# Three shared accumulator banks, a later closing and a third raw buffer in the forgetting stage of a hybrid decoder layer

## The chip, the cores and the metric

The kernel runs on one core of a Trainium2 chip. A core has TensorE (PE in the profile; matmuls, with the loads of their weights on a line of their own, PEld), VectorE (DVE), ScalarE (ACT), GpSimd (POOL) and SyncE (SP), which here only issues DMA transfers. Each engine runs its instructions in the order in which they stand; engines wait for each other by semaphores. Matmuls write to PSUM, which the kernel uses as eight banks of 128 x 512 fp32 numbers; everything else lies in SBUF (on the chip) or in DRAM. The metric is the device time of one execution in microseconds (us), the median of three runs.

## The reference

One decoder layer on a sequence of 1024 tokens with a model width of 1024:

```python
# in outline
h = rmsnorm(x, g)                                  # x (1, 1024, 1024)
q, k, v, ig, fg, fq, fk, fv, ff = split(h @ w_in)   # mLSTM: 4 heads of 128; forgetting attention: 8 heads of 64
a = mlstm_chunkwise(q, k, v, ig, log_sigmoid(fg))   # chunks of 64; q, k behind a causal convolution, a gated and normed
b = forgetting_attention(fq, fk, fv, log_sigmoid(ff))
x = x + concat(a, b) @ w_out
x = x + cross_attention(rmsnorm(x), rmsnorm(mem), w_q, w_kv, w_o)    # 256 memory tokens, 4 heads of 256
x = x + squared_relu_mlp(rmsnorm(x))
return rmsnorm(x, g_final)

def forgetting_attention(q, k, v, lf):              # per block of 128 queries
    s = q @ k.T * 64 ** -0.5
    s = s + (cumsum(lf)[query] - cumsum(lf)[key])   # decay
    s = where(query >= key, s, -inf)
    return softmax(s) @ v
```

All of it is in fp32. The kernel gets that precision by splitting a number into a high part, rounded to the matmul's format, and a low part, the rest; a product is three matmuls (lo x hi, hi x lo, hi x hi).

## The kernel before

The layer runs in stages: the input projections, the mLSTM, the forgetting attention, the output projection with its residual, the cross attention, the MLP, the final norm. The change is in the forgetting stage, which lasts from about 395 to 605 us of the span.

**Work of the stage.** Eight heads, each in two halves of 512 queries. Of a half there are four blocks of 128 queries (class `Tile`), each with its scores against all earlier keys, in parts of at most 512 keys. Per part:

- `score`: two matmuls (L734, L735) of stacked high and low parts into one of three banks `sc`.
- `top`: VectorE's negated row maximum (L741, or L744 with the causal mask).
- `exp`: ScalarE's exponential (L756) with the row's sum as a by-product; where there are two parts a tiny second one (L758).
- `scale`: VectorE makes the reciprocal of the sum (L763, L764), GpSimd multiplies the probabilities by it (L767).

For the output there are 96 value steps (class `Values`), one for each half of a head and each block `j` of 128 keys:

- `turn`: TensorE transposes the probabilities into a bank `tp` (L782).
- `cut`: split of the transposed probabilities into high (ScalarE, L134) and low (VectorE, L135).
- `add`: two matmuls (L801) that add this key block's part of the output to the half's sum. Values are loaded from DRAM (`fvd`, L849).
- `fx_close` when the half is done: the sum's bank holds the output's two parts in its upper and lower 64 partitions; ScalarE copies the upper one to SBUF (L810, `r_c<-ov`) and VectorE adds the lower one to it (L811, `r_f<-ov,r_c`).
- `fx_store` when both heads of a pair are done: the split of the result, and two stores to `mix` (L823, L824).

**Slots.** A function `slot` makes one round of all this: one turn, the adds of the value step two rounds back (`LAG`), the tops of the part that was scored in the round before, the cut, then closings, the exponentials of the parts topped in the round before, the scales, the loads, a score, and then side products. `in_order` fixes that order on every engine, SyncE's issues included: inside the stage nothing overtakes anything on its engine. The score of a slot takes the bank of `sc` whose exponentials stand in the slot before, so TensorE cannot run more than a slot ahead of ScalarE. The value steps follow the scores 13 slots behind (`LEAD_`). Slots are counted here from the first with a value step, which begins with its turn on TensorE.

**Side products.** The rest of a slot's TensorE time goes to matmuls that later stages need, pieced in by a rate (`RATE` 4.6 a slot): keys and values of the cross attention (`key_unit`, `value_unit`) and then the output projection (`out_unit`, 16 units of 128 output columns by 512 tokens, which read the stored `mix` back in pieces, `mix_step`, L934). When a unit is done its `sink` empties its bank a slot later: L885 (keys), L137 and L138 (values), L956 (output projection). Its weights come in raw, by `raw_load` (L975, `wr<-w_out_a`, 320 KB each for the output projection), two buffers `wr` taking turns, and are split in two halves by `cut_half` (L988 ScalarE; L989 the low part, GpSimd for the first half, VectorE for the second). A new raw is asked for in the slot after its buffer was cut.

**Banks.** Three `sc`, two `tp`, one `mm`, one `m2` (in the trace `m`) and one `ov`. In the stage every half's sum is in `ov`, while side products alternate between `mm` and `m2`. In the slot after a closing has been started, no adds are made (`closing`), and the slot after that makes up for them with four; so the next half's sum does not ask for `ov` while the closing reads it.

## Time and profile before

The median of three runs is 1521.66 us (1521.24 to 1523.61).

| | |
|---|---|
| profiled execution, its own time | 1523.35 us |
| its span on the core | 1521.6 us |
| granted TensorE clock | 0.998 |
| TensorE busy, whole span | 1502.7 us |
| VectorE, ScalarE, GpSimd busy | 1100.3, 727.7, 510.1 us |
| forgetting stage, 395 to 605 us: TensorE busy | 204.82 of 210.00 us |
| there VectorE, ScalarE, GpSimd busy | 161.39, 148.75, 94.91 us |

How to read the rows that follow: a row of the timeline has the start, the length, the engine, the line, the operation, what it writes and from what (by the program's names), shapes, and in brackets the idle time of the engine ahead of it and what ended that. Matmuls overlap: the next starts before the former has ended, so a row's length is more than its share of time. A row of a group has the count, then total busy time and mean length in ns, then the idle time ahead of all of its instructions.

### The profile page before, as it was taken

The numbers are of one execution on the slowest core, as the hardware profiler recorded it, in microseconds if no ns is written. First come the engines' busy times: TensorE is split into PE (matmuls) and PEld (weight loads), VectorE is DVE, ScalarE is ACT, GpSimd is POOL, SyncE is SP. The second block draws the span as 40 slices with busy tenths as digits, with TensorE's granted clock in tenths as the row PEclk, the third lists the DMA queues.
The fourth block names the chain that finished last, engine by engine and source line by source line (L and its number), as shares of the span: only waits on it lengthen the run. The fifth ranks groups of instructions, "written<-read, shape, count | busy, mean of one in ns | idle before, by whom it ended". The sixth has DMA issues, their size and how long they took to land.

```text
span 1521.6 us, 21977 instructions
## 1 busy us (share of the span) xinstructions
PE 1502.7 (99%) x7694; PEld 1261.5 (83%) x7694; DVE 1100.3 (72%) x1743; ACT 727.7 (48%) x1360; POOL 510.1 (34%) x543
## 2 busy tenths in 40 slices
PE   9999999999999999999999999999999999999997
PEld 9988888889999788888888877778787888888887
DVE  7766676765787786944457989898887667787665
ACT  7324343334687665644443456666664621122124
POOL 1003030413364442511110034544555265663322
PEclk9999999999999999999999999999999999999999
DMA  6322223435888886843344437776678777776623
GB/s 239 109 77 87 98 100 114 135 126 157 246 244 267 260 264 230 300 131 124 119 147 157 153 134 277 247 256 242 222 252 286 291 277 276 276 270 248 239 94 111
DMA packets 122538, 299.86 MB, mean 197 GB/s; under 512 B 13614, under 2 KB 28264, under 8 KB 115516
## 3 DMA queue, kind: packets, MB, share of 16 engines
q1 hardware_dynamic: 122428, 298.46, 57.4%
q8 instruction: 60, 0.98, 0.3%
q14 instruction: 50, 0.41, 0.1%
HBM read 199.60 MB, written 98.81 MB: 196 GB/s over the span
## 4 chain that ended last, share of the span: by engine, by line
PE 93%; DVE 3%; ACT 2%; DMA 1%; issue 1%; SPq 0%; DVEq 0%; POOLq 0%; POOL 0%; ACTq 0%
PE tp L186 8%; PE tp L187 8%; PE tp L188 8%; PE m L186 6%; PE sc L186 6%; PE m L187 6%; PE m L188 6%; PE sc L187 6%; PE sc L188 6%; PE mm L186 6%; PE mm L187 6%; PE mm L188 6%; PE ov L186 2%; PE ov L187 2%; PE ov L188 2%; PE ov L801 2%
## 5 line engine op out<-in xcount | busy, mean ns | idle before, releaser
L186 PE MATMUL tp<-act,wl 128*128 128x512 f32 (+1 forms) x440 | 172.9, 393 | 1.2 <-ACT row L1396 0.7
L187 PE MATMUL tp<-act,wh 128*128 128x512 f32 (+1 forms) x440 | 172.1, 391 | 0.0
L188 PE MATMUL tp<-act,wh 128*128 128x512 f32 (+1 forms) x440 | 171.7, 391 | 0.0
L135 DVE TENSOR_TENSOR wl<-wr,wh 128x1024 fp32r<-128x1024 f32 (+2 forms) x95 | 124.5, 1311 | 22.0 <-ACT wh L134 21.4
L134 ACT ACTIVATE wh<-wr 128x1024 fp32r<-128x1024 f32 (+2 forms) x95 | 95.6, 1007 | 75.9 <-PE tp L188 34.7
L186 PE MATMUL mm<-act,wl 128*128 128x512 f32 (+1 forms) x332 | 127.5, 384 | 0.0
L188 PE MATMUL mm<-act,wh 128*128 128x512 f32 (+1 forms) x332 | 127.3, 383 | 0.0
L187 PE MATMUL mm<-act,wh 128*128 128x512 f32 (+1 forms) x332 | 127.2, 383 | 0.0
L186 PE MATMUL m<-act,wl 128*128 128x512 f32 (+1 forms) x308 | 117.7, 382 | 0.5 <-DVE wl L135 0.5
L188 PE MATMUL m<-act,wh 128*128 128x512 f32 (+1 forms) x308 | 117.7, 382 | 0.0
L187 PE MATMUL m<-act,wh 128*128 128x512 f32 (+1 forms) x308 | 117.5, 381 | 0.0
L186 PEld LDWEIGHTS tp<-act,wl 128*128 128x128 f32 x440 | 82.6, 188 | 20.6 <-ACT row L1396 1.2
L188 PEld LDWEIGHTS tp<-act,wh 128*128 128x128 f32 x440 | 82.6, 188 | 18.9
L187 PEld LDWEIGHTS tp<-act,wh 128*128 128x128 f32 x440 | 82.7, 188 | 18.5
L186 PE MATMUL sc<-act,wl 128*128 128x512 f32 (+1 forms) x248 | 97.0, 391 | 1.0 <-DVE wl L135 1.0
L188 PE MATMUL sc<-act,wh 128*128 128x512 f32 (+1 forms) x248 | 96.7, 390 | 0.0
L187 PE MATMUL sc<-act,wh 128*128 128x512 f32 (+1 forms) x248 | 96.6, 390 | 0.0
L1467 POOL TENSOR_TENSOR z<-wr 128x256 f32<-128x256 f32 x56 | 51.7, 944 | 130.6 <-DMA wr<-w_ff2q 116.8
L134 ACT ACTIVATE wh<-z 128x1024 fp32r<-128x1024 f32 (+1 forms) x54 | 55.5, 1028 | 80.8 <-POOL z L1467 58.4
L135 DVE TENSOR_TENSOR wl<-z,wh 128x1024 fp32r<-128x1024 f32 (+1 forms) x54 | 74.3, 1376 | 7.8 <-ACT wh L134 7.6
L134 ACT ACTIVATE w<-wr 128x768 fp32r<-128x768 f32 (+2 forms) x31 | 25.5, 823 | 106.2 <-PE tp L186 33.7
L188 PEld LDWEIGHTS mm<-act,wh 128*128 128x128 f32 x332 | 62.3, 188 | 12.7
(726 smaller groups left out, 4288.4 us busy)
## 6 DMA issues: line engine op xcount, KB each, us to landing
act<-right SPq DMA_DIRECT2D x49, 1024.0 KB
right<-w SPq DMA_DIRECT2D x56, 256.0 KB
wr<-w_ff2q SPq DMA_DIRECT2D x28, 512.0 KB
right<-r_d SPq DMA_DIRECT2D x49, 256.0 KB
right<-r_e SPq DMA_DIRECT2D x49, 256.0 KB
act<-fqk SPq DMA_DIRECT2D x48, 256.0 KB
wr<-w_in SPq DMA_DIRECT2D x20, 512.0 KB
wr<-w_ff SPq DMA_DIRECT2D x20, 512.0 KB
```

What stands on the lines that cost most here:

```text
L134: s.activation(hi, src, AF.Copy)
L135: return v.tensor_tensor(out=lo, in0=src, in1=hi.bitcast(F32), op=ALU.subtract)
L186: nc.tensor.matmul(ps, w[1], x[0], start=first, stop=False, skip_group_check=more)
L187: nc.tensor.matmul(ps, w[0], x[1], start=False, stop=False, skip_group_check=more)
L188: nc.tensor.matmul(ps, w[0], x[0], start=False, stop=last, skip_group_check=more)
L801: nc.tensor.matmul(self.ov[:, c0:], self.fv[:, self.j], t[:, c0:], start=self.j == 0 and t is self.p[1], stop=self.last and t is self.p[0])
L1467: g.tensor_tensor(out=o, in0=x, in1=y, op=op)
```

## The change

Three things are changed, all in the forgetting stage.

1. **Banks.** A list `spares` holds `mm`, `m2` and `ov`. The first add of a half and the start of a side product take the bank at its head (`bank_of`); it is put back at its end (`bank_back`) when the closing's addition or the sink has been issued. Adds are no longer left out after a closing: two are made in each slot.
2. **Closing.** ScalarE's copy comes after the exponentials of its slot; VectorE's addition comes in the next slot, after the tops and ahead of the cut. The bank goes back then, and a pair's split and stores come a slot later too.
3. **Raws.** Of the 16 raws of the output projection, numbers 1, 4, 7, 10 and 13 go to a free part of the buffer `row` instead of `wr`. The load of number 0 also issues that of number 1, so that three are under way.

```diff
+    spares, sums = ["mm", "m2", "ov"], {}
+    def bank_of(use):
+        tag = spares.pop(0)
+        sums[use] = ps_tile(tag), tag
+        return sums[use][0]
+    def bank_back(use):
+        spares.append(sums.pop(use)[1])
...
         def add(self):
             c0 = min(self.d0 * P, 256)
+            if self.j == 0:
+                bank_of((self.hd, self.hf))
+            ov = sums[self.hd, self.hf][0]
...
-    def fx_close(hd, hf, ov):
+    def fx_close(hd, hf):
+        ov = sums[hd, hf][0]
...
         s.activation(t[0:FXD], ov[FXD:], AF.Copy)
-        v.tensor_tensor(out=om[hf][rng], in0=ov[0:FXD], in1=t[0:FXD], op=ALU.add)
+        def finish():
+            v.tensor_tensor(out=om[hf][rng], in0=ov[0:FXD], in1=t[0:FXD], op=ALU.add)
+            bank_back((hd, hf))
+            if hd % 2:
+                stores.append((hd, hf, True))
+        return finish
...
-            ps = mm()
+            ps = bank_of("unit")
...
             v.tensor_tensor(out=t[:, 1], in0=ps[:, :NM], in1=row_m, op=ALU.mult)
+            bank_back("unit")
...
-            raw = sb("wr", [P, 1024], 2)[:, : src.shape[-1]]
+            c, m = src.shape[-1], n - len(sources) + 2 * KT
+            raw = row[:, NM : NM + c] if m > 0 and m % 3 == 1 else sb("wr", [P, 1024], 2)[:, :c]
             last_raw[:] = [load(raw, src)]
             raws_.append(raw)
             ages.append(now[1])
+            if m == 0:
+                raw_load()
...
-            closing = bool(ended)
-            ended.clear()
...
-            while adds and not closing and len(adds) >= (LAG if x else 1):
+            while adds and len(adds) >= (LAG if x else 1):
...
             for t, e in tops:
                 t.top(e)
+            while closed:
+                closed.pop(0)()
             if x:
                 x.cut()
                 adds.append(x)
-            for hd, hf, ov in ended:
-                fx_close(hd, hf, ov)
-                if hd % 2:
-                    stores.append((hd, hf, True))
             exps = topped[:]
             topped[:] = tops
             for t, e in exps:
                 t.exp(e)
+            while ended:
+                closed.append(fx_close(*ended.pop(0)))
```

Lines move with it: the turn is L792 after, the add L814, the closing's copy L824, its addition L827, the reads of mix L956, the sinks L905 (keys) and L978 (output projection), the raw's load L999, the first line of a cut half L1014. What each slot holds of side products is the same in both programs.

TensorE in the slot after a closing and the one behind it (slots 14 and 15), before; `tp` are turned probabilities, `r_e` and `r_d` their low and high parts, `ov` the sum, `m` a side product:

```order
L782 MATMUL tp_4275<-ident,w_537_3332 128x128 x2
L734 MATMUL sc_4288<-act_3190 128x512
L735 MATMUL sc_4288<-act_3190 128x512
L186 MATMUL m_683_4220<-act_3833,wl_4136 128x256
L187 MATMUL m_683_4220<-act_3833,wh_4135 128x256
L188 MATMUL m_683_4220<-act_3833,wh_4135 128x256
L782 MATMUL tp_4300<-ident,w_537_3332 128x128
L801 MATMUL ov_4196<-r_e_4206,w_618_3927 128x512
L801 MATMUL ov_4196<-r_d_4205,w_618_3927 128x512
L801 MATMUL ov_4196<-r_e_4245,w_618_3927 128x384
L801 MATMUL ov_4196<-r_d_4244,w_618_3927 128x384
```

The same two slots of TensorE after:

```order
L792 MATMUL tp_4273<-ident,w_537_3332 128x128 x2
L814 MATMUL m_694_4276<-r_e_4205,w_618_3927 128x512
L814 MATMUL m_694_4276<-r_d_4204,w_618_3927 128x512
L734 MATMUL sc_4290<-act_3190 128x512
L735 MATMUL sc_4290<-act_3190 128x512
L186 MATMUL mm_4219<-act_3833,wl_4136 128x256
L187 MATMUL mm_4219<-act_3833,wh_4135 128x256
L188 MATMUL mm_4219<-act_3833,wh_4135 128x256
L792 MATMUL tp_4302<-ident,w_537_3332 128x128
L814 MATMUL m_694_4276<-r_e_4244,w_618_3927 128x384
L814 MATMUL m_694_4276<-r_d_4243,w_618_3927 128x384
```

The first two adds of the new sum have moved a slot forward, ahead of the score, and go to bank `m`; the side product that was in `m` is in `mm`.

ScalarE in a slot with a closing and the next (slots 17 and 18), before; `act<-sc` are the exponentials, `r_c<-ov` the closing's copy, `wh<-wr` half a weight split:

```order
L134 ACTIVATE w_719_4386<-tp_4378 128x512
L810 ACTIVATE r_c_4389<-ov_4196 64x512
L756 ACTIVATE act_4317,c_den_4319<-sc_4320,c_mx_4318 128x512
L988 ACTIVATE wh_4404<-wr_4291 128x512
L134 ACTIVATE r_d_4414<-tp_4408 128x512
L756 ACTIVATE act_4317,c_den_4319<-sc_4362,c_mx_4318 128x128
```

After:

```order
L134 ACTIVATE w_718_4385<-tp_4377 128x512
L756 ACTIVATE act_4317,c_den_4319<-sc_4320,c_mx_4318 128x512
L824 ACTIVATE r_c_4389<-m_694_4276 64x512
L1014 ACTIVATE wh_4402<-wr_4293 128x512
L134 ACTIVATE r_d_4416<-tp_4406 128x512
L756 ACTIVATE act_4317,c_den_4319<-sc_4361,c_mx_4318 128x128
```

The copy has changed places with the exponential; the rest stands as it stood.

SyncE's issues around slots 40 to 44, where the first raws of the output projection are loaded, before; `act<-mix` are pieces of mix that are read back, `act<-fqk` and `act<-decay` a later head's queries and keys, `vxd<-` stores of the cross attention's values:

```order
L975 DMA wr_5199<-w_out_a 128x640
L716 DMA act_3194<-fqk 64x1024
L934 DMA act_5037<-mix 128x512
L716 DMA act_3194<-decay 2x1024
L934 DMA act_5037<-mix 128x512
L908 DMA vxd<-r_b_5254 256x1x256
L975 DMA wr_5293<-w_out_a 128x640
L716 DMA act_3194<-decay 2x1024
```

After:

```order
L999 DMA wr_5198<-w_out_a 128x640
L999 DMA row<-w_out_a 128x640
L716 DMA act_3194<-fqk 64x1024
L956 DMA act_5037<-mix 128x512
L716 DMA act_3194<-decay 2x1024
L956 DMA act_5037<-mix 128x512
L930 DMA vxd<-r_b_5253 256x1x256
L999 DMA wr_5296<-w_out_a 128x640
L716 DMA act_3194<-decay 2x1024
```

A second raw is asked for right behind the first; each later raw stands where its predecessor stood.

More of the change, by code (lines that the diff above doesn't have):

```diff
@@ L799, in add @@
             c0 = min(self.d0 * P, 256)
+            if self.j == 0:
+                bank_of((self.hd, self.hf))
+            ov = sums[self.hd, self.hf][0]
             for t in self.p[::-1]:
-                nc.tensor.matmul(self.ov[:, c0:], self.fv[:, self.j], t[:, c0:], start=self.j == 0 and t is self.p[1], stop=self.last and t is self.p[0])
+                nc.tensor.matmul(ov[:, c0:], self.fv[:, self.j], t[:, c0:], start=self.j == 0 and t is self.p[1], stop=self.last and t is self.p[0])
     om = {}
-    def fx_close(hd, hf, ov):
+    def fx_close(hd, hf):
+        ov = sums[hd, hf][0]
         if hd % 2 == 0:
@@ L898, in run @@
             for t in range(2):
-                ps = mm()[:, :NM]
+                ps = bank_of("unit")[:, :NM]
                 for k in range(KT):
@@ L907, in sink @@
             split(o[:, 0], o[:, 1], ps, rcol_m[:, t : t + 1])
+            bank_back("unit")
             return lambda: void(load(vxd[hd, :, :, t], o.bitcast(F32)))
@@ L949, in run @@
             w = both(ws[0], lambda t: t.rearrange("p (k c) -> p k c", k=MLH + KX))
-            ps = mm()
+            ps = bank_of("unit")
             for k in range(MLH + KX):
@@ L956, in sink @@
             v.tensor_tensor(out=x, in0=ps, in1=x, op=ALU.add)
+            bank_back("unit")
             return lambda: void(load(x1d[hf, :, n], x))
@@ L1019, in hybrid_layer @@
     parts, steps_, fill = score_parts(), value_steps(), filler()
-    scored, exped, adds, ended = [], [], [], []
+    scored, exped, adds, ended, closed = [], [], [], [], []
     spent = [0.0]
@@ L1040, in slot @@
                 if y.last:
[L1041 removed]
+                    ended.append((y.hd, y.hf))
                     break
@@ L1103, in hybrid_layer @@
             cut_for(0)
-    while adds or late or ended or stores:
+    while adds or late or closed or stores:
         n += 1
```

8 lines of the change are left out of this document (3 added, 5 removed).

## The prediction

> **What bounds the kernel now.** I read the page first, then the busy time by stage, then TensorE's rows of the stage with the idle time ahead of each, and for each idle row the engine that released it. From the page, span and busy time:
>
> ```profile
> span 1521.6 us, 21977 instructions
> PE 1502.7 (99%) x7694; PEld 1261.5 (83%) x7694; DVE 1100.3 (72%) x1743; ACT 727.7 (48%) x1360; POOL 510.1 (34%) x543
> ```
>
> TensorE is the bound, and nothing in the change takes work off it. So the change can win only TensorE's idle time in the forgetting stage, or add to it. Busy time of the whole stage, of its crowded part, and of the 35 us behind it:
>
> ```profile
> core 0: us, PE busy (x) PEld busy (x) DVE busy (x) ACT busy (x) POOL busy (x), PEclk, DMA share, GB/s
> 395.00:605.00 210.00, 204.82 (x1282) 179.62 (x1281) 161.39 (x419) 148.75 (x402) 94.91 (x149) 1.00 0.84 251
> 475.00:505.00 30.00, 27.56 (x182) 24.24 (x180) 22.42 (x62) 21.14 (x60) 13.31 (x21) 1.00 1.01 301
> 605.00:640.00 35.00, 35.00 (x156) 28.39 (x155) 32.14 (x36) 22.48 (x35) 18.43 (x13) 1.00 0.80 274
> ```
>
> The stage has 210.00 − 204.82 = 5.18 us of idle TensorE: 0.34% of the run. That is the whole stake on the gain side. TensorE's rows (start, length, and in brackets the idle time ahead and its releaser), in order of time, with some undisturbed rows that I need below:
>
> ```profile
> 428.80 0.39 PE L734 MATMUL sc<-act 128*128 128x512 f32 x1
> 429.03 0.40 PE L735 MATMUL sc<-act 128*128 128x512 f32 x1
> ...
> 430.90 0.39 PE L734 MATMUL sc<-act 128*128 128x256 f32 x1 [1.03 <-ACT act L756]
> 432.60 0.39 PE L734 MATMUL sc<-act 128*128 128x512 f32 x1
> 449.12 0.38 PE L782 MATMUL tp<-ident,w 128*128 128x128 f32 x2
> 449.36 0.50 PE L734 MATMUL sc<-act 128*128 128x512 f32 x1
> 475.99 0.50 PE L734 MATMUL sc<-act 128*128 128x512 f32 x1 [0.49 <-ACT w L756]
> 479.27 0.39 PE L734 MATMUL sc<-act 128*128 128x256 f32 x1 [0.42 <-ACT w L756]
> 485.36 0.60 PE L782 MATMUL tp<-ident,act 128*128 128x128 f32 x4
> 500.53 0.50 PE L187 MATMUL mm<-z,wh 128*128 128x512 f32 x1 [0.34 <-DMA z<-mix]
> 505.14 0.50 PE L734 MATMUL sc<-act 128*128 128x512 f32 x1 [1.33 <-ACT w L756]
> 514.28 0.39 PE L734 MATMUL sc<-act 128*128 128x256 f32 x1 [0.34 <-ACT act L756]
> 531.61 0.50 PE L734 MATMUL sc<-act 128*128 128x512 f32 x1 [0.17 <-ACT w L756]
> 582.18 0.38 PE L782 MATMUL tp<-ident,w 128*128 128x128 f32 x2
> ```
>
> Seven rows wait, 1.03 + 0.49 + 0.42 + 0.34 + 1.33 + 0.34 + 0.17 = 4.12 us; six of them for an exponential on ScalarE (the score of the next slot reuses the bank that the exponential has to empty), one for a transfer. A stall costs more than the idle time shown: undisturbed, the second score matmul starts 429.03 − 428.80 = 0.23 after the first, which is drawn 0.39 long. So each stall costs its idle time and 0.39 − 0.23 = 0.16, and all seven together 4.12 + 7 × 0.16 = 5.24 us.
>
> **The change part by part.** I count slots from the first value slot; a slot begins where TensorE turns the probabilities (L782).
>
> *Copy behind the exponentials (gain).* In the slot in which a head's half closes, ScalarE before and after the closing copy:
>
> ```profile
> 429.45 0.59 ACT L810 ACTIVATE r_c<-ov 64x512 f32<-64x512 f32 x1
> 430.07 0.69 ACT L756 ACTIVATE act<-sc,c_mx 128x512 f32<-128x512 f32 x1
> 430.65 0.19 ACT L756 ACTIVATION_READ_ACCUMULATOR act<-sc,c_mx 128x1 f32 x1
> ...
> 432.00 0.21 ACT L756 ACTIVATION_READ_ACCUMULATOR act<-sc,c_mx 128x1 f32 x1
> 478.55 0.58 ACT L756 ACTIVATE w<-sc,c_mx 128x384 f32<-128x384 f32 x1 [0.81 <-POOL act L767]
> 503.13 0.47 ACT L988 ACTIVATE wh<-wr 128x320 fp32r<-128x320 f32 x1 [2.16 <-DMA wr<-w_out_a]
> ```
>
> At slot 17 the copy (0.59) stands ahead of the exponential for which the score at 430.90 waits 1.03. Behind it, that score comes some 0.6 earlier. But ScalarE has the same work up to the next slot's exponential, whose accumulator is read until 432.00 + 0.21 = 432.21; the score after that, now at 432.60, can start at 432.27 at the earliest (the score at 430.90 starts 0.06 behind its own accumulator read, 430.65 + 0.19 = 430.84). Gain 432.60 − 432.27 = 0.33, not 1.03 + 0.16 = 1.19.
>
> At slots 37 to 40 the chain runs over VectorE and GpSimd:
>
> ```profile
> 475.91 0.67 DVE L811 TENSOR_TENSOR r_f<-ov,r_c 64x512 f32<-64x512 f32 x1
> 476.50 0.20 DVE L763 SCALAR_TENSOR_TENSOR c_den<-c_den,c_mx 128x1 f32<-128x1 f32 x1
> 477.82 0.69 POOL L767 TENSOR_SCALAR act<-act,c_den 128x512 f32<-128x512 f32 x1
> ```
>
> The closing's addition (L811) moves to the next slot, so the denominator (L763) starts 476.50 − 475.91 = 0.59 earlier, with it GpSimd's scaling, which the exponential at 478.55 awaits, and the score at 479.27. The first stall, 475.99, is ahead of that and its loss is contained in the second's. Gain 0.59.
>
> *Third raw buffer (gain).* At 503.13 ScalarE waits 2.16 us for a raw part of w_out_a; the exponential for which TensorE waits at 505.14 stands behind that cut. With three raws under way the cut needs a part that was asked for one unit earlier. Gain 1.33 + 0.16 = 1.49. At 514.28 (the next such place): 0.34 + 0.16 = 0.50. At 531.61, 0.17 + 0.16, I count nothing: there a side product starts on the bank that a sum has given back in the same slot, and waits for the late addition (0.67).
>
> Gains: 0.33 + 0.59 + 1.49 + 0.50 = 2.91 us.
>
> *Adds no longer skipped.* The two adds that were left out of the slot behind a closing are made there, instead of four one slot on; the number stays 64 pairs, so TensorE's work is the same. The group of all adds whose right side comes from the r_e buffers:
>
> ```profile
> L801 PE MATMUL ov<-r_e,w 128*128 128x512 f32 (+2 forms) x64 | 27.2, 426 | 0.0
> ```
>
> No idle time stands ahead of them (0.0): with one bank the skipped slot already hid the closing. Gain nothing. [...]
>
> *Banks in turn (cost).* Before, a sum's bank was emptied by its own closing alone, and side products had two banks of their own. Now a new sum takes whichever of three banks was given back first, and five times (slots 26, 42, 50, 66, 86) that is the bank of a side product whose sink VectorE runs only in the slot before. VectorE at three of them:
>
> ```profile
> 448.85 0.68 DVE L811 TENSOR_TENSOR r_f<-ov,r_c 64x512 f32<-64x512 f32 x1
> 449.90 0.40 DVE L885 TENSOR_TENSOR r_p<-m,row 128x256 f32<-128x256 f32 x1
> 485.57 0.48 DVE L138 SCALAR_TENSOR_TENSOR r_b<-m,rcol_m,r_b 128x256 fp32r<-128x256 f32 x1 [0.19 <-ACT r_b L137]
> 582.87 0.69 DVE L956 TENSOR_TENSOR r_p<-m,r_p 128x512 f32<-128x512 f32 x1
> ```
>
> The add comes behind the turns, whose first matmul starts at 449.12, 485.36 and 582.18 and takes about 0.24 (449.36 − 449.12; four transposes 0.36, an estimate from that). Slot 26: the sink ends at 449.90 + 0.40 = 450.30; the closing's addition ahead of it (0.68) has gone to the next slot, so 449.62, against 449.36: wait 0.25. Slot 42: 485.57 + 0.48 = 486.05, held by ScalarE's half and so not earlier, against 485.72: 0.33. Slot 86: 583.56 less some 0.6 is 582.96 against 582.42: 0.55. At 50 and 66 I find no lag. Cost 0.25 + 0.33 + 0.55 = 1.13. Without the advance, which rests on VectorE doing at once what stands behind the moved addition, the lags are 0.94, 0.33 and 1.14, a mean of 0.80. The addition itself (0.67) now stands ahead of the cut of the next slot; the adds that need this cut come a slot later, some 1.7 us on (432.60 − 430.90), which hides it. If that cover goes, VectorE's sinks are late as well, and it is the bank wait of the second rival.
>
> *Third raw's early transfer (cost).* SyncE's issues, and from the table of transfers the size of a raw part:
>
> ```profile
> 488.68 0.54 SPq L975 DMA_DIRECT2D wr<-w_out_a  x1
> 494.95 0.61 SPq L934 DMA_DIRECT2D z<-mix  x1
> 495.67 0.41 SPq L975 DMA_DIRECT2D wr<-w_out_a  x1
> wr<-w_out_a SPq DMA_DIRECT2D x16, 320.0 KB
> ```
>
> The load that goes with the first raw is issued ahead of the pieces of mix, for the last of which TensorE waits at 500.53. The DMA engines are full there (share 1.01, 301 GB/s), so 320 KB ahead in the queue are 327,680 B / 301 GB/s = 1.09 us later at 500.53, if nothing else gives way. The issues move with the slots, so what TensorE has won by then (0.33 + 0.59, less the waits of 0.25 + 0.33) stays won, and the landing is 1.09 − 0.34 = 0.75 later than before. Cost 1.09. Its ends: 0, if the transfer finds spare share as in the stage's 0.84; 2.18, twice as much, if it takes turns with a neighbour and delays both. I take the middle, since the row nearest to the place is the full one. The stores of a finished pair (mix<-) also go one slot later on SyncE's queue, behind two reads of mix; nothing in the stage waits for them, and the reads they let pass gain no more than the same 1.09, which is inside the two ends.
>
> *Sum.* 2.91 − 1.13 − 1.09 = 0.69 us net gain. The profiled execution took 1523.35 (its span 1521.6 and 1.7 around it), 1.69 above the median 1521.66 of the runs shown (1521.24 to 1523.61). A gain of 0.69 inside the span is one off the median too: 1521.66 − 0.69 = 1521.0. Its own range: transfer hidden and no bank wait, 1521.66 − 2.91 = 1518.8, say 1519.0; bank waits of 0.94 + 0.33 + 1.14 = 2.41 and transfer at 2.18, 1521.66 + 1.68 = 1523.3.
>
> **The rivals.**
>
> *Faster than that: all seven stalls go.* The early load costs nothing and each stall is removed whole: 5.24 − 1.13 = 4.11, so 1517.5. For it: six of the seven stalls hang on ScalarE's exponentials, and three kinds of delay ahead of these are moved. Against it: the work of ScalarE up to the next exponential is unchanged (slot 17), and the DMA share is 1.01 where the transfer is added. [...]
>
> *Slower: the turn of the banks becomes the wait.* Eight places take a bank given back in the slot before or the same one: five new sums and three side products (slots 30, 62, 78). If VectorE's sink ends later than 0.36 behind the start of the turns at all of them, with the mean lag 0.80, 8 × 0.80 = 6.4 us; with the transfer's 1.09 and the gains of 2.91, 4.6 slower: 1526.2. For it: VectorE has 22.42 of 30 us busy in the crowded part, and the moved addition puts 0.67 ahead of the cuts. Against: three of the five sums were worked out at 0.25 to 0.55 and two at nothing.
>
> *No change of the stage, but one behind it.* The scheduler orders the instructions behind the stage a little differently; there VectorE is busy 32.14 of 35 and TensorE all 35.00. A group of VectorE's, 1.1 to 2 us long, that comes late eats the gain: about 1523.
>
> **How the numbers follow.** A measurement of this kernel can tell 0.2%, 3.0 us, from no change: 1518.6 to 1524.7. My forecast (1519.0 to 1523.3) has a chance of 0.47, since each of its terms but the banks' has a row of its own, and lies within; the rival behind the stage 0.12, within. All stalls gone 0.24, faster; banks 0.17, slower. So 0.24, 0.59, 0.17. The range holds 8 in 10 if it takes the best of the faster rival (1517.5, just inside) and most of the slower one, short of its full 1526.2: 1517.4 to 1525.5.
>
> **What would show it.** Idle rows of the score at slots 18, 40, 50 and 54 gone or under 0.2; new idle rows ahead of the first add of a sum at slots 26, 42 and 86, released by VectorE, of 0.25 to 0.55; the wait for the last piece of mix near slot 48 grown from 0.34 to about 1.4; idle of TensorE in the stage at about 4.5. The prediction is wrong if the wait for mix does not grow (the transfer was free), if waits for banks stand at eight places, or if idle rows appear behind the stage.

## The result: 0.25% slower, and the profile after

The changed kernel takes 1525.79 us in the median of eight runs (1524.18 to 1527.88), the kernel before 1521.68 (1521.08 to 1523.61). The ratio is 1.0025, with a 95% interval of 1.0015 to 1.0036. In a second comparison it was 1.0016 (1.0008 to 1.0025). So it is slower, by the ratios 2.4 to 3.8 us, where 0.7 us of gain was forecast; 1525.79 lies just above the range.

The busy time of the stage in the profile of the changed kernel (profiled execution 1525.0 us, span 1523.3):

```profile
core 0: us, PE busy (x) PEld busy (x) DVE busy (x) ACT busy (x) POOL busy (x), PEclk, DMA share, GB/s
395.00:605.00 210.00, 204.85 (x1286) 179.08 (x1285) 162.51 (x417) 147.26 (x400) 96.09 (x149) 1.00 0.85 249
475.00:505.00 30.00, 28.78 (x200) 25.66 (x199) 24.16 (x64) 22.84 (x63) 16.54 (x24) 1.00 1.03 305
605.00:640.00 35.00, 35.00 (x157) 28.46 (x156) 28.58 (x35) 21.45 (x34) 16.41 (x12) 1.00 0.72 252
```

TensorE idles 210.00 − 204.85 = 5.15 us in the stage, as much as the 5.18 before. The 35 us behind it are full, as before. The idle rows have changed places. TensorE's rows with idle time ahead, of the changed kernel, in order of time:

```profile
397.86 0.55 PE L792 MATMUL tp<-ident,w 128*128 128x128 f32 x3 [0.56 <-DVE r_b L138]
402.22 0.39 PE L734 MATMUL sc<-act 128*128 128x256 f32 x1 [0.42 <-ACT w L756]
409.61 0.33 PE L792 MATMUL tp<-ident,act 128*128 128x128 f32 x1 [0.51 <-DVE r_e L135]
426.93 0.36 PE L186 MATMUL ov<-act,wl 128*128 128x256 f32 x1 [0.41 <-DVE r_f L827]
434.86 0.50 PE L734 MATMUL sc<-act 128*128 128x512 f32 x1 [0.71 <-ACT act L756]
452.20 0.50 PE L814 MATMUL ov<-r_e,w 128*128 128x512 f32 x1 [0.33 <-DVE r_p L905]
457.76 0.50 PE L734 MATMUL sc<-act 128*128 128x512 f32 x1 [0.43 <-ACT w L756]
481.15 0.33 PE L792 MATMUL tp<-ident,act 128*128 128x128 f32 x1 [0.36 <-DVE w L135]
503.94 0.50 PE L187 MATMUL ov<-z,wh 128*128 128x512 f32 x1 [0.71 <-DMA z<-mix]
533.93 0.50 PE L186 MATMUL mm<-act,wl 128*128 128x512 f32 x1 [0.21 <-DVE r_f L827]
584.42 0.50 PE L814 MATMUL mm<-r_e,w 128*128 128x512 f32 x1 [0.32 <-DVE r_p L978]
```

The first two rows, at slots 1 and 4, stand in the kernel before as well (0.52 and 0.41). The stalls at slots 50 and 54 (1.33 and 0.34) are gone and the others for the exponential are smaller. In their place TensorE waits for VectorE: for cuts (L135), for banks that wait for the closing's addition (L827), for banks that wait for a sink (L905, L978). These waits answer to the second rival by their places, but the experiments show that the turn of the banks alone is not what makes them.

### The profile page after: what moved, and what is told of

The parts are those of the page before. It is cut to its first block, busy times and chain, and to the rows that moved or that the text cites. A ratio compares the mean times of both kernels' runs of the same rounds, so it can differ in the third digit from the quotient of the medians.

```text
span 1523.3 us, 21974 instructions
## 1 busy us (share of the span) xinstructions
PE 1502.9 (99%) x7694; PEld 1260.9 (83%) x7694; DVE 1099.3 (72%) x1743; ACT 726.4 (48%) x1360; POOL 510.6 (34%) x543
## 4 chain that ended last, share of the span: by engine, by line
PE 90%; DMA 4%; DVE 3%; ACT 1%; issue 1%; SPq 0%; POOL 0%; DVEq 0%; POOLq 0%; ACTq 0%
PE tp L186 8%; PE tp L187 8%; PE tp L188 8%; PE sc L186 6%; PE sc L187 6%; PE sc L188 6%; PE mm L186 6%; PE mm L187 6%; PE mm L188 6%; PE m L186 5%; PE m L187 5%; PE m L188 5%; PE ov L186 3%; PE ov L187 3%; PE ov L188 3%; PE tp L792 1%
## 5 line engine op out<-in xcount | busy, mean ns | idle before, releaser
L135 DVE TENSOR_TENSOR wl<-wr,wh 128x1024 fp32r<-128x1024 f32 (+2 forms) x95 | 123.5, 1300 | 24.9 <-ACT wh L134 24.5
L186 PE MATMUL mm<-act,wl 128*128 128x512 f32 (+1 forms) x312 | 120.5, 386 | 0.2 <-DVE r_f L827 0.2
L187 PE MATMUL mm<-act,wh 128*128 128x512 f32 (+1 forms) x312 | 120.3, 386 | 0.0
L188 PE MATMUL mm<-act,wh 128*128 128x512 f32 (+1 forms) x312 | 120.2, 385 | 0.0
L186 PE MATMUL m<-act,wl 128*128 128x512 f32 (+1 forms) x284 | 109.9, 387 | 0.5 <-DVE wl L135 0.5
L188 PE MATMUL m<-act,wh 128*128 128x512 f32 (+1 forms) x284 | 110.1, 388 | 0.0
L187 PE MATMUL m<-act,wh 128*128 128x512 f32 (+1 forms) x284 | 109.9, 387 | 0.0
L135 DVE TENSOR_TENSOR wl<-z,wh 128x1024 fp32r<-128x1024 f32 (+1 forms) x54 | 73.8, 1367 | 7.8 <-ACT wh L134 7.6
L186 PEld LDWEIGHTS mm<-act,wl 128*128 128x128 f32 x312 | 58.6, 188 | 12.5 <-DVE r_f L827 0.6
```

Of the source, the lines that this page charges most:

```text
L135: return v.tensor_tensor(out=lo, in0=src, in1=hi.bitcast(F32), op=ALU.subtract)
L186: nc.tensor.matmul(ps, w[1], x[0], start=first, stop=False, skip_group_check=more)
L187: nc.tensor.matmul(ps, w[0], x[1], start=False, stop=False, skip_group_check=more)
L188: nc.tensor.matmul(ps, w[0], x[0], start=False, stop=last, skip_group_check=more)
```

## The experiments

The theories that the expectations name: A, the turn of the banks loses the time; B, the third raw's early transfer does; C, the loss lies outside the stage; and, added after the first four experiments, D, the closing's addition a slot later does.

Each ratio is to the kernel before, run on the same chip side by side, with a 95% interval. The medians of the kernel before went from 1521.7 to 1523.0 between such comparisons, so ratios are compared and not medians. To place a loss I use the times at which TensorE starts the turns of slots 0, 37, 60 and 95. In the profiles of the kernel before and the changed kernel these stretches read:

| us | slots 0 to 37 | 37 to 60 | 60 to 95 |
|---|---|---|---|
| before, first and second profile | 78.69, 78.71 | 53.62, 52.45 | 70.79, 70.79 |
| changed, first and second profile | 80.37, 80.40 | 51.66, 54.49 | 71.56, 71.52 |

The outer stretches repeat within 0.04 us, and there the changed kernel loses 1.7 and 0.75, together 2.4 us, the lower of the two measured losses. The middle one, where the DMA engines are full (share 1.01 and 1.03 from 475 to 505 us), differs from run to run by 1 to 3 us; in the first profile of the changed kernel it happened to be short, and so hides most of the loss.

### Undoing one part

*Without the early load* (1.0021; 1.0012 to 1.0030). The stretches: 80.65, 52.37, 71.53.

```diff
-            if m == 0:
-                raw_load()
```

> The changed kernel, but the load of the first raw part no longer issues the second one as well; the third buffer is there, one load fewer is under way. Changed kernel 1525.8, kernel before 1521.7. Theory A (the turn of the banks loses the time: new idle rows of TensorE at first adds of sums and at side products): the waits for banks stay, the wait of 1.5 for the weight part at slot 50 comes back and about 0.4 of the wait for mix goes: 1526.9. Theory B (the early transfer loses it, here and in other transfers): 1522 to 1523.5. Theory C (the loss lies outside the stage, where the two programs differ only in order and place of code): 1525.8 plus 1.1, as A, but with the loss visible ahead of 395 us or behind 605 us in this profile too.

The wait for mix is gone, a wait at slot 50 is there (1.48, for a sink), and the time is not lower than the changed kernel's by what can be told. Theory B in its simple form falls; the expected loss of 1.1 us is not seen either.

*Sums in a bank of their own* (1.0052; 1.0040 to 1.0064). The stretches: 83.60, 54.40, 71.26.

```diff
-    spares, sums = ["mm", "m2", "ov"], {}
+    free = {"unit": ["mm", "m2"], "sum": ["ov"]}
...
-            while adds and len(adds) >= (LAG if x else 1):
+            while adds and not closed and len(adds) >= (LAG if x else 1):
```

> The changed kernel, but sums only in the bank ov, side products only in mm and m2, and no adds in the slot after a closing, as before. Copy, late addition and third raw buffer stay. Theory A: the five rows in which TensorE waited for a bank in the changed kernel (0.57 + 0.50 + 0.31 + 0.38 + 0.48 = 2.24) go, so 1523.5, and if the timed runs lose more to them than the profiled one, down to 1521.7. Theory B: no change, 1525.8. Theory C: 1523.5, but idle rows outside the stage stay.

This contradicts all three theories: without the turn of the banks the loss doubles. The late addition gives `ov` back a slot later, and the adds that make up for the skipped slot now wait for the addition (L828 in this kernel), as TensorE's row in slot 7 shows:

```profile
408.19 0.47 PE L815 MATMUL ov<-r_e,w 128*128 128x512 f32 x1 [1.36 <-DVE r_f L828]
```

The turn of the banks hides part of what the late addition costs.

*The closing's copy ahead of the exponentials again* (1.0032; 1.0020 to 1.0045). The stretches: 80.43, 52.71, 71.87.

```diff
+            while ended:
+                closed.append(fx_close(*ended.pop(0)))
             exps = topped[:]
             topped[:] = tops
             for t, e in exps:
                 t.exp(e)
-            while ended:
-                closed.append(fx_close(*ended.pop(0)))
```

> The changed kernel, but the closing's copy stands ahead of the exponentials again; its addition stays a slot later, banks and raws stay changed. All theories: the stall at slot 18 comes back (1.19), the one at slot 20 (0.87, new in the changed kernel) may go: 1526.1, give or take 0.8. If it is faster than the changed kernel by over 1 us, the moved copy itself loses time, which none of A, B and C says.

As expected within the interval: the moved copy does not lose time.

*The addition in the slot of its copy, behind the scales* (1.0007; 0.9997 to 1.0018). The stretches: 79.15, 52.53, 71.76.

```diff
             while exped:
                 exped.pop(0).scale()
+            while ended:
+                fx_close(*ended.pop(0))()
```

(with the two lines behind the exponentials taken out)

> The changed kernel (banks in turn, three raws, early load), but the closing's addition is made in the slot of its copy, behind the scales, and the bank goes back then. Theory D (the addition a slot later loses the time): slots 0 to 37 back from 80.4 to about 78.7, slots 60 to 95 from 71.5 to 70.6, so 2.5 less than the changed kernel: 0.1% over the kernel before or less. Theory A (the turn of the banks): slots 0 to 37 stay above 80, the whole at 0.2% over. If raws cost 2 us by themselves (theory B), slots 37 to 60 stay at 52 to 54.5.

Theory D is met in the total and in the first stretch (1.2 of 1.7 us come back), but not in the last, which stays at 71.8: an addition behind the scales with banks in turn still makes some sums wait.

*The late addition behind the cut* (1.0036; 1.0023 to 1.0049). The stretches: 81.53, 53.19, 73.69.

```diff
-            while closed:
-                closed.pop(0)()
             if x:
                 x.cut()
                 adds.append(x)
+            while closed:
+                closed.pop(0)()
```

> The changed kernel, but the late addition stands behind the cut of its slot instead of ahead of it. By theory D with the order as the cause, the turns that wait for a cut (0.64 at slot 8, 0.53 at slot 39) lose their wait, and the waits for the bank that the addition gives back (0.57 at slot 15, 0.37 at slot 63) grow by up to 0.7: no gain in sum, within 0.5 us of the changed kernel. If the whole loss lies in the cut's place, 1.5 us less than the changed kernel.

Slower still, by more than was expected; its interval overlaps that of the first comparison of the changed kernel, but the outer stretches lose 1.2 and 2.1 us more. The waits for cuts went, and the waits for the bank grew (0.74 and 0.69 us of idle time in place of 0.41 and 0.21), with two more of 1.52 at places where the changed kernel had none. Neither place in that slot is free: ahead of the cut the addition delays the turns, behind it the bank.

### One part alone

*Banks in turn alone* (0.9998; 0.9989 to 1.0007). The changed kernel's code for the banks, two raw buffers, and the closing as before:

```diff
             while ended:
-                closed.append(fx_close(*ended.pop(0)))
+                fx_close(*ended.pop(0))()
```

(moved ahead of the exponentials)

> The kernel before with the turn of the three banks alone (adds no longer left out); the closing's copy and addition stand where they stood before, two raw buffers. Kernel before 1521.9. Theory A (the turn of the banks itself loses): the waits for a sink at slots 26, 42 and 86 are there (0.50 + 0.31 + 0.48 in the changed kernel), so 1523 or more. Theory D (the loss of the first 37 slots, 1.7 in the changed kernel's profile, comes from the late addition, which stands ahead of cuts and holds a bank a slot longer): slots 0 to 37 as before, 78.7, and the whole 1522 to 1522.5.

Theory A falls here. The turn of the banks alone costs nothing and brings nothing. Its row at slot 26 shows why: the new sum goes to `mm`, which the closing has just given back, 0.09 behind the turn's end. In the changed kernel that bank is not back yet, and the sum takes `ov` from a side product's sink and waits 0.33 (452.20, above).

```profile
449.31 0.38 PE L792 MATMUL tp<-ident,w 128*128 128x128 f32 x2
449.78 0.50 PE L814 MATMUL mm<-r_e,w 128*128 128x512 f32 x1
```

*Banks in turn and late addition, no third raw* (1.0018; 1.0008 to 1.0027).

```diff
-            c, m = src.shape[-1], n - len(sources) + 2 * KT
-            raw = row[:, NM : NM + c] if m > 0 and m % 3 == 1 else sb("wr", [P, 1024], 2)[:, :c]
+            raw = sb("wr", [P, 1024], 2)[:, : src.shape[-1]]
...
-            if m == 0:
-                raw_load()
```

> The changed kernel without the third raw buffer and without the early load: banks in turn and the closing in two slots. The kernel before with the raws alone took 2.6 more than before, the changed kernel 3.9 to 4.1 more. If the costs of the parts add up, 1521.9 + 1.3 to 1.5 = 1523.2 to 1523.4. If banks and closing lose the time and the raws only hide or show it, 1525 or more. The stretch of slots 0 to 37 should read 80.4 to 80.7 as in the changed kernel, in either case.

This kernel and banks in turn alone differ in the closing alone. TensorE's turns of slots 0, 37, 60 and 95 with banks in turn alone:

```profile
395.08 0.27 PE L792 MATMUL tp<-ident,w 128*128 128x128 f32 x1
...
473.90 0.27 PE L792 MATMUL tp<-ident,w 128*128 128x128 f32 x1
...
527.16 0.27 PE L792 MATMUL tp<-ident,w 128*128 128x128 f32 x1
...
597.92 0.27 PE L792 MATMUL tp<-ident,act 128*128 128x128 f32 x1
```

and with the late closing besides:

```profile
396.01 0.27 PE L792 MATMUL tp<-ident,w 128*128 128x128 f32 x1
...
476.50 0.27 PE L792 MATMUL tp<-ident,w 128*128 128x128 f32 x1
...
533.19 0.27 PE L792 MATMUL tp<-ident,w 128*128 128x128 f32 x1
...
604.77 0.27 PE L792 MATMUL tp<-ident,act 128*128 128x128 f32 x1
```

The outer stretches go from 473.90 − 395.08 = 78.82 to 476.50 − 396.01 = 80.49, and from 597.92 − 527.16 = 70.76 to 604.77 − 533.19 = 71.58: 1.67 and 0.82 us, which is the changed kernel's loss there. The middle stretch of this profile (56.69), the longest of twelve executions, has waits for transfers and is one draw. By the ratios the late closing costs 0.0020, some 3.0 us.

VectorE ahead of the turn of slot 8 shows how. First the changed kernel, then banks in turn alone:

```profile
407.69 0.68 DVE L741 TENSOR_REDUCE c_mx<-sc 128x1 f32<-128x512 f32 x1
408.29 0.67 DVE L827 TENSOR_TENSOR r_f<-mm,r_c 64x512 f32<-64x512 f32 x1
408.88 0.67 DVE L135 TENSOR_TENSOR r_e<-tp,r_d 128x512 fp32r<-128x512 f32 x1
```

```profile
406.82 0.68 DVE L741 TENSOR_REDUCE c_mx<-sc 128x1 f32<-128x512 f32 x1
407.42 0.67 DVE L135 TENSOR_TENSOR r_e<-tp,r_d 128x512 fp32r<-128x512 f32 x1
```

The addition takes 0.59 us of VectorE's queue (408.88 − 408.29) between the maximum and the cut. The turn two slots later needs the cut's bank `tp`, and there are two of these. In the changed kernel it waits 0.51 (409.61, above). The stretches of a few slots agree. Against the kernel before, banks in turn alone lose −0.02, −0.14 and 0.17 us at slots 6 to 8, 14 to 16 and 29 to 33; with the late closing besides 0.36, 0.51 and 0.65.

*Third raw alone* (1.0011; 1.0003 to 1.0020). The stretches: 79.15, 54.69, 70.76.

```diff
+            c, m = src.shape[-1], n - len(sources) + 2 * KT
+            raw = row[:, NM : NM + c] if m > 0 and m % 3 == 1 else sb("wr", [P, 1024], 2)[:, :c]
...
+            if m == 0:
+                raw_load()
```

> The kernel before with the third raw buffer and the early second load alone. Theory A: the stalls at slots 50 and 54 go (1.50 + 0.50), the wait for mix grows by 0.4: 1520.1. Theory B: 1523 to 1525, most of the loss. Theory C: 1520.1 or, if any shift of the program disturbs what lies outside, 1521 to 1524 with idle rows ahead of 395 us.

Slower where a gain of 1.6 us was expected by theory A. In its profile ScalarE waits 3.38 us for the first raw (1.39 in the first profile of the kernel before), TensorE therefore 1.44 at slot 45, and 1.11 for mix. The stall at slot 50 is gone; the one at slot 54, which the prediction put down to a raw, stays as it was (0.34):

```profile
493.91 0.47 ACT L991 ACTIVATE wh<-wr 128x320 fp32r<-128x320 f32 x1 [3.38 <-DMA wr<-w_out_a]
```

```profile
503.92 0.51 PE L187 MATMUL mm<-z,wh 128*128 128x512 f32 x1 [1.11 <-DMA z<-mix]
516.06 0.39 PE L734 MATMUL sc<-act 128*128 128x256 f32 x1 [0.34 <-ACT act L756]
```

### The closing moved otherwise

*Closing behind the exponentials and scales of its own slot, alone* (0.9984; 0.9975 to 0.9992), and once more (0.9986; 0.9978 to 0.9995).

```diff
-            for hd, hf, ov in ended:
-                fx_close(hd, hf, ov)
-                if hd % 2:
-                    stores.append((hd, hf, True))
             exps = topped[:]
...
             while exped:
                 exped.pop(0).scale()
+            for hd, hf, ov in ended:
+                fx_close(hd, hf, ov)
+                if hd % 2:
+                    stores.append((hd, hf, True))
```

> The kernel before with one change: the closing's copy and addition both stand behind the exponentials and the scales of their own slot; sums stay in ov, adds are left out for a slot as before, two raw buffers. The step of the prediction on the closing: stalls at slots 18 and 40 go, 0.33 + 0.59, so 1521.0. Rival: what waited for the exponential waits for the next thing on ScalarE or VectorE, and nothing is won: 1521.9. If the addition now comes too late for the four adds two slots on, a wait of 0.3 to 1 at each of fifteen closings: 1526 or more.

> The closing behind the exponentials and scales of its own slot, alone, once more: 0.16% under the kernel before, as the first time, with idle TensorE in slots 37 to 60 of 1.5 us or less.

This beats both kernels, by 2.1 to 2.4 us, more than the 0.9 that was worked out. The busy time in the second of its profiles, and two rows of TensorE:

```profile
395.00:605.00 210.00, 207.01 (x1302) 182.35 (x1302) 162.48 (x422) 150.31 (x405) 94.73 (x149) 1.00 0.86 254
```

```profile
432.39 0.50 PE L801 MATMUL ov<-r_e,w 128*128 128x512 f32 x1 [0.40 <-DVE r_f L811]
...
478.06 0.50 PE L801 MATMUL ov<-r_e,w 128*128 128x512 f32 x1 [0.59 <-DVE r_f L811]
```

Idle TensorE in the stage is 2.99 us. The adds wait for the addition at two places (0.40 and 0.59), where the stall for the exponential stood, so the first stretch stays as it was (78.74 and 78.71). The gain is behind: the middle stretch is 50.45 and 50.46, twice the same, with no wait of TensorE for a raw or for mix, and the last 70.36 and 70.33 (70.79 before). Against the second profile of the kernel before it stands at four places, each in or behind a slot with a closing: 0.38 at slots 37 to 41, 1.02 at 50 to 52, 0.60 at 54 to 56 and 0.44 at 62 to 64. ScalarE in slot 53 shows the cause, first the kernel before, then this one:

```profile
512.83 0.60 ACT L810 ACTIVATE r_c<-ov 64x512 f32<-64x512 f32 x1
513.45 0.69 ACT L756 ACTIVATE act<-sc,c_mx 128x512 f32<-128x512 f32 x1
```

```profile
511.21 0.68 ACT L756 ACTIVATE act<-sc,c_mx 128x512 f32<-128x512 f32 x1
...
512.01 0.60 ACT L810 ACTIVATE r_c<-ov 64x512 f32<-64x512 f32 x1
```

The copy stood ahead of the exponential for which TensorE waits at slot 54. In slot 49 it stood in the same way (504.01 in the first profile) between the cut that waits for a raw (503.13) and the exponential (504.63) for which TensorE waits at slot 50, so some 0.6 of that stall was the copy's too. Why the raw for slot 49 also came in time in both runs (ScalarE waited 2.16 and 0.96 for it before) is open; it is not that the loads start earlier, since the first raw is asked for 87.33 and 87.66 us behind the first turn, against 86.85 and 87.25.

*The same with banks in turn* (0.9999; 0.9989 to 1.0009). Stretches 79.20, 50.86, 71.52.

```diff
             while exped:
                 exped.pop(0).scale()
+            while ended:
+                fx_close(*ended.pop(0))()
```

(in the kernel with banks in turn and two raws)

> Banks in turn, closing behind the exponentials and the scales of its own slot, two raws as before. The closing alone behind took 0.16% off the kernel before, the banks alone nothing. Theory D: as the closing alone or better, because its two waits for the late addition at slots 19 and 39 (0.56 + 0.82) have no place where the sums take another bank: 0.15 to 0.25% under the kernel before. Theory A: 0.1% over.

Banks in turn take the gain back: sums that start in the next slot wait for the addition, 0.73 at slot 26.

*The same with the third raw, sums in `ov`* (0.9998; 0.9988 to 1.0008). Stretches 78.79, 50.45, 70.36.

```diff
+            raw = row[:, NM : NM + c] if m > 0 and m % 3 == 1 else sb("wr", [P, 1024], 2)[:, :c]
...
+            if m == 0:
+                raw_load()
```

> The kernel before with the closing behind the exponentials and the scales of its own slot, and with the third raw buffer and the early load; sums in ov. Theory B: the raws cost what they cost alone, 0.1 to 0.17%, so level with the kernel before, with waits for mix or for a raw of 1 us or more in slots 37 to 60. If the raws only shift chance waits about: 0.1 to 0.2% under, as the closing alone.

The time is as theory B has it, but the profile, one of the shorter executions, shows no wait for a raw or for mix in the middle stretch, only the 0.59 for the addition at slot 39 that stands without the raws too. The differences between pairs of kernels point the same way, weakly: the raws cost 0.0011 alone, 0.0012 to 0.0014 here, 0.0008 beside banks in turn and same-slot closing, and −0.0002 to 0.0007 beside the late closing.

### The transfer by itself

*The extra load behind the last piece of mix* (1.0019; 1.0010 to 1.0028). Stretches 80.52, 50.96, 71.49.

```diff
-            if m == 0:
+            if m == 2:
                 raw_load()
```

> The changed kernel, but the extra load goes with the third raw of the output projection instead of the first, and so stands behind the last piece of mix on SyncE's queue. In eight profiles with the early load TensorE waited in seven for that piece (0.7 to 2.1 us), in six without it once (0.34). If the place of the transfer ahead of mix causes that wait: no wait, or 0.3 at most, for mix in slots 46 to 50, and about 1 us less than the changed kernel, 0.12% over the kernel before. If any third raw under way costs the same: the wait goes elsewhere and the time stays at 0.16 to 0.25% over.

The wait for mix is gone, the middle stretch is the shortest of all kernels with the late addition, and the time is where it was (the profile is of the shortest of twelve executions). So the place ahead of mix makes that wait, and the wait does not decide the median.

*A transfer of 320 KB alone* (1.0004; 0.9996 to 1.0013). Stretches 79.09, 54.34, 70.77.

```diff
             last_raw[:] = [load(raw, src)]
+            if n - len(sources) + 2 * KT == 0:
+                load(row[:, NM : NM + src.shape[-1]], src)
```

> The kernel before, with one more transfer of 320 KB (a second copy of the first raw, into a free part of row, which nothing reads) at the place where the changed kernel issues its early load; nothing else. The disputed cost by itself: 1.1 us later for the last piece of mix by the sum of the prediction, so a wait of 1.1 to 1.4 there and 0.07% over the kernel before. If it is hidden: 0.3 as before, and no difference.

TensorE waits 0.59 us for mix (0.34 before), not 1.1 to 1.4, and elsewhere 0.45 and 0.99 for exponentials. The measured 0.04% excludes neither nothing nor the estimated 0.07%.

*The two kernels once more.* The kernel before gave 1.0002 (0.9992 to 1.0012) against itself.

> The changed kernel once more, unaltered, for a second profile beside its kin: 1525.8. If the idle rows ahead of 395 us (1.56 more than before in the first profile) are there again, they belong to the program; if not, they are chance. The wait for the last piece of mix should differ between the two profiles if transfers decide it (0.71 in the first; 1.11 to 1.85 in three variants).

> The kernel before once more, for a second profile: 1521.7 to 1523. If its waits for the raw at slot 50 (1.33) and for mix (0.34) are the rule and not chance, they are there again within 0.5 us.

In the second profile of the kernel before the stage's idle TensorE is 4.27 us, not 5.18. Its stage and its wait at slot 50:

```profile
395.00:605.00 210.00, 205.73 (x1289) 180.64 (x1288) 162.01 (x419) 150.16 (x405) 95.35 (x149) 1.00 0.84 253
```

```profile
504.42 0.50 PE L734 MATMUL sc<-act 128*128 128x512 f32 x1 [0.75 <-ACT w L756]
```

The wait for mix does not appear in it. In the second profile of the changed kernel mix makes TensorE wait 2.14 us, three times the first. The first turn came at 396.46 in the first and at 394.39 in the second (394.81 and 395.24 before): what it had lost ahead of the stage was chance, and theory C falls.

## Why the prediction was wrong, point by point

The steps can be read off from how far each slot's turn is behind the same turn of the kernel before, in the two profiles that were compared first:

| step | forecast, us | measured, us | the same slots in other runs |
|---|---|---|---|
| copy behind the exponentials, slots 18 to 20 | −0.33 | −0.25 | copy ahead of them again −0.24; banks in turn alone −0.25 |
| addition out of the chain, slots 37 to 41 | −0.59 | −0.67 | banks in turn alone 0.00 |
| third raw, slots 50 to 52 | −1.49 | −1.43 | third raw alone −1.59; closing behind alone −1.59 |
| third raw, slots 54 to 56 | −0.50 | −0.61 | third raw alone 0.00; closing behind alone −0.61 |
| sinks at slots 26, 42, 86 | +1.13 | +0.33 + 0.38 + 0.57 = +1.28 | banks in turn alone +0.06 − 0.03 + 0.38 = +0.41 |
| wait for mix, slots 48 to 49 | +1.09 | +0.37 | without the early load −0.61 |
| not foreseen: slots 6 to 8, 14 to 16, 29 to 33 | 0 | +0.38 + 0.57 + 0.65 = +1.60 | banks in turn alone 0.0 |

Each gain and each wait for a sink came out within 0.12 us, but for three of these rows the last column shows another mechanism than the forecast's, and there the agreement is luck. At slots 18 to 20 the gain is the same without the moved copy: banks in turn put two adds ahead of the score that waited, and its wait goes from 1.03 to 0.57 in banks in turn alone. At slots 54 to 56 the third raw alone gains nothing; the stall was the copy's. And the sums at slots 26 and 86 take a sink's bank only when the late addition keeps back the one that the closing would have returned; at slot 86 0.38 of the 0.57 is lost without that too. At slots 50 to 52 the third raw alone removes the stall, as forecast, but so does the closing behind the exponentials, so these two gains do not add up. Two steps failed.

**The late addition was costed at nothing.** The step said that the addition "now stands ahead of the cut of the next slot; the adds that need this cut come a slot later … which hides it". The adds were covered. But the cut also empties a bank `tp` that a later turn needs (slot 8, a wait of 0.51), and the bank of the sum comes back a slot later, for which a side product waits (slots 15 and 62, 0.41 and 0.21; the prediction had charged slot 62 with it, by leaving out its gain, and not slot 15). At slots 29 to 33 the score waits for a later exponential (457.76, a wait of 0.43): with the addition, ScalarE's split of the finished pair (0.63 us, at 455.40) has gone a slot later too, and now stands close ahead of that exponential. To this comes some 0.9 us of the sinks' 1.28. Three pairs of kernels that differ in the late closing give its price: 0.9998 to 1.0018; 0.9999 to 1.0018 where copy and addition stand in the same slot behind the scales; and, with the third raw, 1.0007 to 1.0025 or 1.0016. That is 0.0009 to 0.0020, 1.4 to 3 us, against the forecast net gain of 0.7. The time came close to the second rival's 1526.2, but that is luck, since its mechanism did not hold: banks in turn alone cost nothing, and with late additions they save (1.0052 without them).

**Gains were read from one draw and taken off the median.** The profiled execution of the kernel before was 1.69 above the median of the runs. The prediction saw that and still subtracted gains worked out from that execution. Its stall of 1.33 at slot 50 is 0.75 in the second profile, and its wait for mix is absent there. The gain of 1.49 is 0.75 + 0.16 = 0.91 by that one. Two smaller readings were off as well: nine rows wait in the stage and not seven (0.52 at slot 1 and 0.41 at slot 4 are missing), so that 5.24 lies close to 5.18 by chance; and the 64 adds of the row shown are a third of the 192, not 64 pairs. Neither enters the sum of 0.69.

**The transfer's price** (1.09, ends 0 and 2.18) was of the right kind. In nine profiles with the early load, or such a transfer alone, ahead of mix, TensorE waited for mix in eight, 0.59 to 2.14 us; in nine without one it waited once, 0.34. But taking that wait away did not change the time (1.0019). That the third raw costs time is shown, narrowly, where it stands alone (1.0003 to 1.0020); in the other pairs the difference is 0 to 0.14%, and their intervals overlap. By which wait it costs in the usual run is open.

The first rival, all stalls gone, failed at its own condition, that the turn of the banks and the new order add no waits. TensorE's wait at slot 50 (1.33) went, but with the DMA engines full (share 1.03 from 475 to 505 us) the early transfer was not free for its neighbour: in eight of nine profiles TensorE waited for mix, 0.59 to 2.14 us. That it also delayed the first raw is not shown: ScalarE's wait for that raw lies between nothing and 3.38 us in the nine profiles with the early transfer, and between nothing and 2.30 in the nine without. The rival behind the stage did not occur: TensorE is busy all 35.00 us there, as before.

## What to carry to other kernels

When several users share buffers in turn, the one that gives its buffer back later also changes which buffer the others get. Moving a last read one step later may free one engine's queue and still cost at several other places (here 0.38, 0.57 and 0.65 us at slots 6 to 8, 14 to 16 and 29 to 33, for an addition drawn 0.67 long), so list every resource that the delayed step gives back (here the bank of the sum, and behind the delayed cut the bank of the turn) and who asks for each next. Moving work behind the critical instruction of its own step (copy and addition behind the exponentials and scales) won 0.15% where moving it into the next step, with banks in turn, lost 0.1 to 0.2%. Where transfers filled the DMA engines (share 1.01 and 1.04 from 475 to 505 us in two profiles of the kernel before), the stalls in one profile were a draw (1.33 and 0.75 at slot 50; 0.34 and none for mix): price a gain from two profiles, or from one that lies at the median. A gain of the forecast size is no proof of the forecast cause: look whether it is still there when the part is left out.

## What the runs showed of the hardware

A long stall cost more than its length here. In the second profile of the changed kernel TensorE waits 2.14 us for mix, and the matmuls behind it start 0.42 to 0.43 apart instead of 0.23. TensorE's rows, and the stretches with the granted clock:

```profile
503.42 0.79 PE L187 MATMUL ov<-z,wh 128*128 128x512 f32 x1 [2.14 <-DMA z<-mix]
504.01 0.63 PE L188 MATMUL ov<-z,wh 128*128 128x512 f32 x1
504.44 0.84 PE L792 MATMUL tp<-ident,w 128*128 128x128 f32 x3
...
506.15 0.63 PE L186 MATMUL mm<-act,wl 128*128 128x512 f32 x1
506.57 0.43 PE L187 MATMUL mm<-act,wh 128*128 128x512 f32 x1
506.85 0.40 PE L188 MATMUL mm<-act,wh 128*128 128x512 f32 x1
507.08 0.39 PE L186 MATMUL mm<-act,wl 128*128 128x512 f32 x1
```

```profile
501.00:503.00 2.00, 0.28 (x2) 0.00 (x0) 1.23 (x3) 1.43 (x5) 0.99 (x2) 1.00 0.84 269
503.00:505.00 2.00, 1.58 (x6) 1.28 (x6) 0.35 (x2) 0.00 (x0) 0.00 (x0) 0.56 1.08 291
505.00:507.00 2.00, 2.00 (x9) 1.86 (x8) 1.12 (x4) 1.65 (x5) 0.09 (x1) 0.59 1.07 293
507.00:509.00 2.00, 2.00 (x12) 1.60 (x11) 1.92 (x6) 0.95 (x5) 2.00 (x3) 1.00 1.03 215
```

The granted clock is 0.56 and 0.59 in the two stretches behind the stall, from 503 to 507 us, and 1.00 from 507. With banks in turn and late closing alone a wait of 2.39 (ended at 510.26) was followed by clocks of 0.51 and 0.63, from 511 to 513 and from 513 to 515 us. Behind a wait of 2.08 (banks in turn alone) it stayed at 1.00:

```profile
505.65 0.50 PE L814 MATMUL m<-r_e,w 128*128 128x512 f32 x1 [2.08 <-DVE r_f L827]
505.99 0.39 PE L814 MATMUL m<-r_d,w 128*128 128x512 f32 x1
506.22 0.39 PE L734 MATMUL sc<-act 128*128 128x512 f32 x1
506.45 0.39 PE L735 MATMUL sc<-act 128*128 128x512 f32 x1
```

The price can be read from the turns: slots 48 to 50 of the profile with 2.14 take 7.80 us (499.98 to 507.78), 3.87 more than in the second profile of the kernel before, 1.7 more than the wait itself. Slots 50 to 52 with the wait of 2.08 take 2.35 more than where no wait stands there, 0.3 more than the wait.
